# An encoder trunk of two layers: the order of tasks and weight splits chosen by an account of time at build, and a bank of its own for the last 128 columns

## The chip, the cores and the metric

The kernel runs on one core of one Trainium2 chip. The metric is the device time of one execution in microseconds (us); the number given for the kernel before is the median of three runs. TensorE is called PE below, VectorE DVE, ScalarE ACT, GpSimd POOL, and SyncE, which issues the weight loads, SP.

## The reference

```python
D_MODEL = 1024; BATCH = 1; SEQ = 256; DEPTH = 2
HEAD_DIM = 64; D_FF = 2816; GRID_W = 64; WINDOW = 128
...
def swiglu(h, w_gate, w_up, w_down):
    return (jax.nn.silu(h @ w_gate) * (h @ w_up)) @ w_down
...
def even_mixer(h, w_in, q_gain, k_gain, sink, w_out, rope1, rope_axial):
    proj = h @ w_in
    ...
    qa = apply_axial_rope(rms_norm(qa, q_gain), *rope_axial)
    ka = apply_axial_rope(rms_norm(ka, k_gain), *rope_axial)
    oa = global_gqa(qa, ka, va)
    qb = apply_rope(qb, *rope1)
    kb = apply_rope(kb, *rope1)
    ob = windowed_gqa_sink(qb, kb, vb, sink)
    return jnp.concatenate([oa, ob], axis=-1) @ w_out
...
    for layer in range(DEPTH):
        i = layer // 2
        h = rms_norm(x, ffn1_norm[layer])
        x = x + 0.5 * swiglu(h, ffn1_w_gate[layer], ffn1_w_up[layer], ffn1_w_down[layer])
        h = rms_norm(x, mix_norm[layer])
        if layer % 2 == 0:
            x = x + even_mixer(h, even_w_in[i], a_q_norm[i], a_k_norm[i], b_sink[i],
                               even_w_out[i], rope1, rope_axial)
        else:
            x = x + odd_mixer(h, odd_w_qkv[i], c_rel_bias[i], odd_w_out[i], rows)
        h = rms_norm(x, ffn2_norm[layer])
        x = x + 0.5 * swiglu(h, ffn2_w_gate[layer], ffn2_w_up[layer], ffn2_w_down[layer])
    return rms_norm(x, final_norm)
```

The odd mixer is attention within a clamped neighbourhood of a grid of tokens, 16 heads, with a learned bias that is looked up by the relative place. All inputs are float32.

## The kernel before

The 256 tokens are two tiles of 128 rows (`tt` 0 and 1), and `x` stays on chip. There are six stages: feed-forward, even mixer, feed-forward, feed-forward, odd mixer, feed-forward with the final normalisation.

**Products.** Each product of 128 rows of a weight with a tile is done in three matmuls (a triple): each operand is split into a high part and a rest, and high by high, high by rest and rest by high are added (`mm`, L382 to L384). A raw weight block is loaded by SP into one of three buffers (L299). ACT makes its high part `hi` (L390), DVE the rest `lo` (L393). `wp` holds seven such split blocks. The activations are transposed by PE (into banks `tp`) and split in the same way: `th`, `tl` for the normalised `x` (L437, L422), `g_h`, `g_l` for the gated product (L459), `qTb`, `kTaz` and the like for the heads.

**Order.** The engines' lists for PE, ACT, DVE and SP stand as the program is written out. POOL's list is ordered by the framework's own scheduler. Side work (a gated product, a rope, a pair of heads) is a generator, called a task. `tick` runs after each triple; a task says after how many triples it goes on, by numbers written by hand:

```python
GLU_WAIT = 5
KA_WAITS = [2, 5]
EVEN_WAITS = {'a': [[2, 3, 4, 0], [0, 3, 3, 1, 1, 0]], 'b': [[2, 3, 2, 0], [0, 3, 2, 0, 0, 1]]}
```

Weight splits are put in at a fixed number per triple (`RATE` and the like), at most seven blocks ahead; a product whose split isn't made yet makes it on the spot.

**Feed-forward** (`ffn`). Gate and up projections come in chunks of 512 or 384 columns, tile by tile; ACT makes `silu`, DVE the gated product `glu` (L574), and after `GLU_WAIT` triples PE transposes it. The down projection is partly done by Strassen's seven products (`seven`, and `combine`, L671 to L697, whose additions DVE does one by one). The last four blocks of 128 rows of the down projection are held back and done half by half (`use`), so that the additions to `x` (L511) follow each other. In the last stage the second tile's second half is done as 384 and 128 columns, both in one bank `s`.

**Even mixer** (`even`, `attend`). Keys and values of both groups are projected first (bank `s`), then group B's queries (`pj`), then group A's. Keys are rotated by POOL (`kra` for group A, `krb` for B, L869 and L886), then transposed by PE (L933); queries are rotated by DVE (`qr`, L884) and transposed (L459). `pair` then does two heads for each call: scores (L793, L794), maxima by DVE, exponentials by ACT, normalisation by POOL, transposes of `p` (L857) and a copy to `pt` (L753), and the product with the values (L778).

**Odd mixer** (`odd`). The same with `okTz` and `oqT`; POOL builds the bias tables (L1025) from rows that SP loads, DVE adds them to the scores in the pass that takes the maxima (L811), and DVE normalises.

**The end** (`after`). POOL and DVE multiply by the last gain (L1124, L1128), DVE adds up the squares (L1114), POOL raises to the power (L1118), ACT and DVE scale (L1132, L1133), and two queues store.

## Time and profile before

| | us |
|---|---|
| runs | 973.82, 973.82, 975.64 |
| median | 973.82 |
| the profiled execution | 973.97 |
| its span in the trace | 972.2 |
| PE busy | 954.7 |
| DVE busy | 686.2 |
| ACT busy | 554.3 |
| POOL busy | 87.9 |

The profiled execution's own time is 1.77 us longer than its span, which lies outside of what the trace shows. "Busy" is the time in which an engine's records run; PE's matmul records overlap, so PE can be busy all the time and still be fed. A wait is idle time of an engine just before an instruction, with the instruction of another engine that released it. Times within the trace count from the start of the span.

### The profile page before, as it was taken

To read this page: it belongs to the slowest core of one execution; us is meant where nothing else is said; L and a number is where in the kernel's file an instruction comes from. 1 tells how busy PE (TensorE), PEld (TensorE's weight loads), DVE (VectorE), ACT (ScalarE), POOL (GpSimd) and SP (SyncE) were. 2 spreads that over 40 slices of the span, in tenths; PEclk is the share of its full clock that TensorE was granted. 3 is DMA by queue.
4 is the path that set the end of the run, shared out by engine and by line. 5 is a ranking of instruction groups with operands and counts; after the bars stand their busy time and mean duration, and the time that the engine had idled before them with its cause. 6 is when DMAs were issued, how large, how long until landed. Compare 5 with 4: busy or idle time off the path is not lost.

```text
span 972.2 us, 12895 instructions
## 1 busy us (share of the span) xinstructions
PE 954.7 (98%) x4806; PEld 805.7 (83%) x4806; DVE 686.2 (71%) x1095; ACT 554.3 (57%) x960; POOL 87.9 (9%) x152
## 2 busy tenths in 40 slices
PE   9999999998999999999999999999999999999996
PEld 6888998877778888988888899888878888889885
DVE  6665679878857565688866557887869676656796
ACT  7554465576677454555655444648877565445550
POOL 1020000063420000000000000003312000000002
PEclk9999999999999999999999999999999999999998
DMA  8675556563226554646555546465554355545451
GB/s 278 197 254 163 176 191 238 179 174 88 87 87 202 188 171 154 212 160 243 187 174 189 172 158 216 176 257 172 169 158 143 128 176 195 186 158 185 184 195 44
DMA packets 82368, 171.66 MB, mean 177 GB/s; under 512 B 3712, under 2 KB 25216, under 8 KB 82304
## 3 DMA queue, kind: packets, MB, share of 16 engines
q1 hardware_dynamic: 81728, 170.23, 52.9%
q8 instruction: 38, 0.62, 0.3%
q10 hardware_dynamic: 576, 0.59, 0.2%
q14 instruction: 26, 0.21, 0.1%
HBM read 169.76 MB, written 1.05 MB: 176 GB/s over the span
## 4 chain that ended last, share of the span: by engine, by line
PE 93%; ACT 3%; DVE 2%; issue 1%; POOL 1%; DMA 0%; POOLq 0%; ACTq 0%
PE pj L382 14%; PE pj L384 14%; PE pj L383 14%; PE s L382 12%; PE s L384 12%; PE s L383 12%; PE tp L459 3%; PE o L384 2%; PE o L383 2%; PE o L382 2%; PE o L778 1%; PE tp L857 1%; PE tp L437 1%; PE s L793 1%; ACT hi L390 1%
## 5 line engine op out<-in xcount | busy, mean ns | idle before, releaser
L393 DVE TENSOR_TENSOR lo<-raw,hi 128x1024 fp32r<-128x1024 f32 (+2 forms) x388 | 384.1, 1013 | 140.4 <-ACT hi L390 136.6
L390 ACT ACTIVATE hi<-raw 128x1024 fp32r<-128x1024 f32 (+2 forms) x388 | 328.3, 879 | 131.3 <-PE pj L384 106.5
L382 PE MATMUL pj<-hi,th 128*128 128x512 f32 (+1 forms) x512 | 198.4, 388 | 0.0
L384 PE MATMUL pj<-hi,tl 128*128 128x512 f32 (+1 forms) x512 | 193.3, 377 | 0.0
L383 PE MATMUL pj<-lo,th 128*128 128x512 f32 (+1 forms) x512 | 192.9, 377 | 0.1
L382 PE MATMUL s<-hi,th 128*128 128x512 f32 (+1 forms) x400 | 152.5, 381 | 0.0
L384 PE MATMUL s<-hi,tl 128*128 128x512 f32 (+1 forms) x400 | 149.6, 374 | 0.0
L383 PE MATMUL s<-lo,th 128*128 128x512 f32 (+1 forms) x400 | 149.3, 373 | 0.0
L384 PEld LDWEIGHTS pj<-hi,tl 128*128 128x128 f32 x512 | 96.3, 188 | 15.6
L383 PEld LDWEIGHTS pj<-lo,th 128*128 128x128 f32 x512 | 96.7, 189 | 13.4 <-DVE lo L393 0.5
L382 PEld LDWEIGHTS pj<-hi,th 128*128 128x128 f32 x512 | 96.6, 189 | 13.1 <-issue 0.3
L384 PEld LDWEIGHTS s<-hi,tl 128*128 128x128 f32 x400 | 75.4, 188 | 11.1
L383 PEld LDWEIGHTS s<-lo,th 128*128 128x128 f32 x400 | 75.6, 189 | 10.5
L382 PEld LDWEIGHTS s<-hi,th 128*128 128x128 f32 x400 | 75.6, 189 | 10.2
L402 POOL TENSOR_TENSOR rstd<-var,mhalf 128x1 f32<-128x1 f32 (+2 forms) x16 | 15.3, 959 | 586.0 <-ACT th L422 310.2
L574 DVE SCALAR_TENSOR_TENSOR glu<-pj,rstd,silu 128x512 f32<-128x512 f32 (+1 forms) x48 | 33.7, 703 | 41.8 <-PE pj L384 41.8
L382 PE MATMUL s<-hi,g_h 128*128 128x512 f32 (+2 forms) x116 | 45.5, 392 | 2.3 <-DVE x L511 2.3
L384 PE MATMUL s<-hi,g_l 128*128 128x512 f32 (+2 forms) x116 | 44.7, 385 | 0.0
L383 PE MATMUL s<-lo,g_h 128*128 128x512 f32 (+2 forms) x116 | 44.5, 384 | 0.0
L393 DVE TENSOR_TENSOR g_l<-tp,g_h 128x384 fp32r<-128x384 f32 (+1 forms) x48 | 28.8, 599 | 20.8 <-ACT g_h L390 20.8
L390 ACT ACTIVATE shi<-raw 128x1024 fp32r<-128x1024 f32 x16 | 17.0, 1061 | 43.5 <-DVE raw L315 43.5
L422 ACT ACTIVATE th<-tp,mats 128x128 fp32r<-128x128 f32 x88 | 25.2, 371 | 24.7 <-PE tp L437 21.4
(351 smaller groups left out, 1372.2 us busy)
## 6 DMA issues: line engine op xcount, KB each, us to landing
raw<-in_ffn_w_down SPq DMA_DIRECT2D x44, 1024.0 KB, 5.0
raw<-in_ffn_w_up SPq DMA_DIRECT2D x32, 1024.0 KB, 5.1
raw<-in_ffn_w_gate SPq DMA_DIRECT2D x30, 1024.0 KB, 5.1
raw<-in_ffn_w_gate SPq DMA_DIRECT2D x16, 768.0 KB, 4.4
raw<-in_ffn_w_up SPq DMA_DIRECT2D x16, 768.0 KB, 4.5
raw<-in_odd_w_qkv SPq DMA_DIRECT2D x12, 1024.0 KB, 5.1
raw<-in_even_w_in SPq DMA_DIRECT2D x4, 1024.0 KB, 6.3
raw<-in_even_w_out SPq DMA_DIRECT2D x8, 512.0 KB, 5.8
```

The costliest lines, as they stand in the source:

```text
L382: mm(ps, h, wh, start=first, stop=False)
L383: mm(ps, h, wl, start=False, stop=False)
L384: mm(ps, l, wh, start=False, stop=last)
L390: self.nc.scalar.activation(hi, src, AF.Copy)
L393: self.nc.vector.tensor_tensor(lo, src, hi.bitcast(F32), op=ALU.subtract)
L402: nc.gpsimd.tensor_tensor(r[:, :n], v[:, :n], self.mhalf[:, :n], op=ALU.pow)
L422: self.nc.scalar.activation(hi, tb[:, j * P : j * P + P], AF.Copy, scale=gain)
L437: nc.tensor.transpose(tb[:, j * P : (j + 1) * P], self.x[tt][:, b * P : (b + 1) * P], self.ident)
L459: self.nc.tensor.transpose(tb[:, i * P : (i + 1) * P], src[:, i * P : (i + 1) * P], self.ident)
L574: nc.vector.scalar_tensor_tensor(m[:, :w], u[:, :w], self.now.r[tt], s[:, :w], op0=ALU.mult, op1=ALU.mult)
L778: self.nc.tensor.matmul(O[64 * s : 64 * s + 64, i * P : i * P + P], v(b0 + i, s, kc), pT[s][:, i, kc, :], start=(kc == 0), stop=(kc == 1),)
L793: nc.tensor.matmul(S[:, i, :], q, kz[s], start=True, stop=False)
```

## The change

The numbers written by hand go. A class `Clock` reads the instructions as they are written out and adds up rough times for each engine (`cost`, `catch_up`), with the times at which operands are written and buffers come free. A task now yields a `Need`: the engine that goes on with it, the operands it waits for, and a condition. `may` lets it go on when the account has the operands ready: for PE 150 ns ahead of PE's own time, for the others within 400 ns after. `tick` looks at all tasks after each triple; when a triple can't go on, `tick` adds 100 ns of idle PE to the account and tries again. Weight splits are put in whenever there is room and the account has the raw block there (`supply_now`). Banks are counted (`open`, `done`, `has`), and a wait for a bank is one of the conditions.

The second part: where columns 896 to 1024 of the last tile are done apart, their held-back products go to a bank `tp` (`to`), and the addition for 512 to 896 takes in all 512 columns of the bank `s`, with what had been added up before for the last 128; those get a second addition from `tp`. The engines have as many instructions as before, kind by kind.

```diff
 FIT = {"wp": 7, "sum": 3}
-RATE = 0.53
-DOWN_RATE = 0.78
-EVEN_RATE = 0.48
-ODD_RATE = 0.51
+FEW = 4
 
 HELD = 2
 
-X_WAIT = 5
-R_WAIT = 3
-GLU_WAIT = 5
-NAT_WAIT = 2
-ROPE_WAIT = 3
-KB_WAIT = 6
-KA_WAITS = [2, 5]
-QA_WAIT = 9
-EVEN_GAP = {'a': 2, 'b': 2}
-ODD_GAP = [4, 3]
-EVEN_WAITS = {'a': [[2, 3, 4, 0], [0, 3, 3, 1, 1, 0]], 'b': [[2, 3, 2, 0], [0, 3, 2, 0, 0, 1]]}
-ODD_WAITS = [[[2, 4, 5, 4], [2, 4, 5, 3, 1, 2]], [[0, 4, 4, 4], [4, 3, 3, 5, 0, 2]]]
+
+EARLY = 150
+WAIT = 400
+REACH = 1000
...
+class Clock:
...
+        if e == "PE":
+            dt = inst.ins[0].dtype
+            if dt == F32R:
+                t = 9 + 0.426 * n
+            elif dt == F32:
+                t = 109 * n / 128
+            else:
+                t = 0.426 * n
+            return t, t + 165
+        if e == "ACT":
+            t = max(255, 40 + 1.04 * n) + (190 if len(outs) > 1 else 0)
+            return t, t + 70
+        m = n
+        for x in ins:
+            k = 1
+            for _, c in x.ap[1:]:
+                k *= c
+            m = max(m, k)
+        if e == "DVE":
+            return 90 + 1.04 * m, 150 + 1.04 * m
+        t = 650 + 140 * (m - 1) if m <= 8 else 250 + (2.2 if len(ins) > 1 else 1.1) * m
+        return t, t + 20
...
+            begin = max([self.at[e]] + [self.last(self.written, x, e) for x in ins] + [self.last(self.used, x, e) for x in outs])
+            self.at[e] = begin + busy
...
+class Need:
+
+
+    def __init__(self, engine, operands, when=lambda: True, soon=False):
+        self.engine, self.operands, self.when = engine, operands, when
+        self.soon = soon or engine in ("PE", None)
...
+    def has(self, tag):
+
+        if self.open[tag] == BANKS[tag]:
+            return False
+        return self.clock.next_free("acc", tag, BANKS[tag]) + EARLY <= self.clock.at["PE"]
...
+    def may(self, need):
+
+        at = self.clock.at
+        if not need.when():
+            return False
+        if need.engine is None:
+            return True
+        t = self.clock.ready(need.operands)
+        if need.engine == "PE":
+            return t + EARLY <= at["PE"]
+        if at[need.engine] > at["PE"] + REACH:
+            return False
+        return t <= max(at["PE"], at[need.engine]) + WAIT
+
+    def await_parts(self, parts):
+        while self.clock.ready([t for part in parts for t in part]) > self.clock.at["PE"]:
+            self.tick(True)
 
     def finish(self, task):
         while task[1] is not None:
-            self.tick(False)
-
-    def tick(self, supply=True):
-        self.low()
+            self.tick(True)
+
+    def tick(self, idle=False):
+
+        self.clock.catch_up()
+        if idle:
+            self.clock.at["PE"] += 100
+            self.idle += 1
+            assert self.idle < 1000, [task[0] for task in self.tasks]
+        else:
+            self.idle = 0
+        if self.half is not None and self.may(self.need("DVE", self.half[0].parts[0][:, self.half[1]])):
+            self.low()
         for task in list(self.tasks):
-            task[0] -= 1
-            if task[0] <= 0 and task[1] is not None:
-                self.step(task)
-        if supply:
-            self.due += self.rate
-            n = self.whole[0].step() if self.whole else 1
-            if self.due >= n and self.room():
-                self.due = min(self.due - n, n)
-                self.supply()
+            if isinstance(task[0], int) and not idle:
+                task[0] -= 1
+                if task[0] <= 0:
+                    self.step(task)
+            self.go_on(task, True)
+        if sum(self.live.values()) <= FEW:
+            self.supply_now()
+        for task in list(self.tasks):
+            self.go_on(task, False)
+        self.supply_now()
+
+    def go_on(self, task, soon):
+        while task[1] is not None and isinstance(task[0], Need) and (task[0].soon or not soon) and self.may(task[0]):
+            self.step(task)
+
+    def supply_now(self):
+        if self.room() and self.may(self.need("ACT", self.whole[0].raw)) and self.clock.at["DVE"] <= self.clock.at["PE"] + REACH:
+            self.supply()
+            self.clock.catch_up()
...
-            yield GLU_WAIT
+            self.done("pj")
             n = w // P
+            yield self.need("PE", m[:, :w], when=lambda: self.has("tp"))
...
-        def use(f, tt, sl, last=False):
+        def use(f, tt, sl, last=False, to=None):
             while f not in gT[tt]:
-                self.tick(False)
+                self.tick(True)
+            self.await_parts([gT[tt][f]])
             i = sl.start // 512
             at = slice(sl.start % 512, (sl.stop - 1) % 512 + 1)
-            self.mm(Y[tt][i][:, at], gT[tt][f], W[f][i], (tt, i) not in begun, last, at, at.start > 0)
+            ps = Y[tt][i][:, at] if to is None else to[:, : sl.stop - sl.start]
+            self.mm(ps, gT[tt][f], W[f][i], (tt, i) not in begun if to is None else f == held[0], last, at)
...
+                to = self.bank("tp") if sl.start > 512 else None
                 for f in held:
-                    use(f, tt, sl, f == held[-1])
-                at = slice(sl.start % 512, (sl.stop - 1) % 512 + 1)
-                self.start(self.add_to_x(tt, sl, Y[tt][sl.start // 512][:, at], 0.5))
-
-
-    def attend(self, qT, has_q, kT, v, has_v, tag, dest, gap, waits, norm, sink=None, bias=None, scale=None):
+                    use(f, tt, sl, f == held[-1], to)
+                i = sl.start // 512
+                tag = ("o", "pj")[i] if tt == 0 else "s" if to is None else "tp"
+                ps = Y[tt][i] if to is None else to[:, : sl.stop - sl.start]
+                self.start(self.add_to_x(tt, sl, ps, 0.5, tag=tag))
...
-            yield KB_WAIT
+            yield self.need("PE", kr, when=lambda: self.has("tp"))
...
-                    while not has_q(tt):
-                        yield 1
-                    self.start(pair(tt, b0, s))
-                    yield gap
-        while len(dest[NT - 1]) < 4:
-            yield 1
+                    yield self.need(None, when=lambda: qT(tt) is not None and kT(0) is not None)
+                    own = [qT(tt)[b0 + i][s] for i in range(2)] + [kT(b0 + i)[j][s] for i in range(2) for j in range(2)]
+                    yield self.need("PE", *own, when=lambda: self.has("s"))
+                    self.start(pair(n, tt, b0, s))
+                    n += 1
```

How the lists move is shown at three places; line numbers of the changed kernel differ (L565 to L567 are its `mm`, L1154 its transpose of keys).

**Even mixer.** PE's list before, in the first query projection of group B (`pj_2028`), up to the transpose of group A's keys of the first tile (`kra_1969`); this is behind six triples of that projection, of which the last three are shown.

```order
L382 MATMUL pj_2028<-hi_1873,th_1770 128x512
L383 MATMUL pj_2028<-lo_1874,th_1770 128x512
L384 MATMUL pj_2028<-hi_1873,tl_1771 128x512
L382 MATMUL pj_2028<-hi_1926,th_1812 128x512
L383 MATMUL pj_2028<-lo_1927,th_1812 128x512
L384 MATMUL pj_2028<-hi_1926,tl_1813 128x512
L382 MATMUL pj_2028<-hi_1926,th_1815 128x512
L383 MATMUL pj_2028<-lo_1927,th_1815 128x512
L384 MATMUL pj_2028<-hi_1926,tl_1816 128x512
L933 MATMUL tp_2081<-mats,kra_1969 128x128
```

The same place in the changed kernel, from the first product of the projection (there `pj_2032`, and `kra_1967`).

```order
L565 MATMUL pj_2032<-hi_1851,th_1748 128x512
L566 MATMUL pj_2032<-lo_1852,th_1748 128x512
L567 MATMUL pj_2032<-hi_1851,tl_1749 128x512
L565 MATMUL pj_2032<-hi_1851,th_1751 128x512
L566 MATMUL pj_2032<-lo_1852,th_1751 128x512
L567 MATMUL pj_2032<-hi_1851,tl_1752 128x512
L565 MATMUL pj_2032<-hi_1933,th_1754 128x512
L566 MATMUL pj_2032<-lo_1934,th_1754 128x512
L567 MATMUL pj_2032<-hi_1933,tl_1755 128x512
L1154 MATMUL tp_2063<-mats,kra_1967 128x128
```

The transpose stands three triples earlier. POOL's list there before, from the rotation of `ka` of the first tile to its sum `kra`; `kb_2037` is the other group's keys of the second tile, and `kTbx` a copy of transposed keys.

```order
L869 TENSOR_TENSOR t_2_478_2019<-ka_1968,gtab 128x128
L869 TENSOR_TENSOR t_2_479_2020<-ka_1968,gtab 128x2x16 x4
L489 CAST kTbx_425_1851<-kTbz_423_1849 64x128
L489 CAST kTbx_426_1852<-kTbz_424_1850 64x128
L869 TENSOR_TENSOR t_2_483_2041<-kb_2037,tab 128x128
L869 TENSOR_TENSOR t_2_484_2042<-kb_2037,tab 128x2x32 x2
L886 TENSOR_TENSOR kra_1969<-t_2_478_2019,t_2_479_2020 128x128
```

And POOL's list in the changed kernel, from the two copies on:

```order
L682 CAST kTbx_434_1866<-kTbz_432_1864 64x128
L682 CAST kTbx_435_1867<-kTbz_433_1865 64x128
L1150 TENSOR_TENSOR ka_1966<-ka_1966,rstd_1984 128x128
L1089 TENSOR_TENSOR t_2_472_1987<-ka_1966,gtab 128x128
L1089 TENSOR_TENSOR t_2_473_1988<-ka_1966,gtab 128x2x16 x4
L1089 TENSOR_TENSOR t_2_483_2041<-kb_2037,tab 128x128
L1089 TENSOR_TENSOR t_2_484_2042<-kb_2037,tab 128x2x32 x2
L1106 TENSOR_TENSOR kra_1967<-t_2_472_1987,t_2_473_1988 128x128
```

The copies of `kTbx` moved up by three places; the two products from `kb_2037` stand ahead of `kra` in both.

**Odd mixer.** DVE's list before, from the first group's first pair of scores on: `s_6547` is the first pair's scores, `bias_6264` and `bias_6270` the first two tables, `oqT_1556` the split of the second tile's queries.

```order
L811 ISA p_6568,m_6567<-s_6547,bias_6264 128x256
L811 ISA m_6567 128x1
L811 ISA p_6568,m_6567<-s_6547,bias_6270 128x256
L811 ISA m_6567 128x1
L816 TENSOR_SCALAR m_1554_6571<-m_6567 128x2
L393 TENSOR_TENSOR lo_6561<-raw_6115,hi_6560 128x512
L393 TENSOR_TENSOR oqT_1556_6586<-tp_6576,oqT_1556_6586 64x512
L393 TENSOR_TENSOR oqT_1557_6587<-tp_6576,oqT_1557_6587 64x512
```

In the changed kernel, from the second pair of scores on (the first stands just ahead), with the second and third pair's scores (`s_6564`, `s_6570`) and the third and fourth table (`bias_6291`, `bias_6297`):

```order
L1031 ISA p_6584,m_6583<-s_6564,bias_6279 128x256
L1031 ISA m_6583 128x1
L1031 ISA p_6584,m_6583<-s_6564,bias_6285 128x256
L1031 ISA m_6583 128x1
L1036 TENSOR_SCALAR m_1560_6587<-m_6583 128x2
L1031 ISA p_6590,m_6589<-s_6570,bias_6291 128x256
L1031 ISA m_6589 128x1
L1031 ISA p_6590,m_6589<-s_6570,bias_6297 128x256
L1031 ISA m_6589 128x1
L1036 TENSOR_SCALAR m_1563_6593<-m_6589 128x2
L576 TENSOR_TENSOR oqT_1566_6608<-tp_6598,oqT_1566_6608 64x512
```

The pass with the third and fourth table now stands ahead of the split of `oqT`; it came later before.

**The end.** DVE's last additions to `x` before, from the second tile's first half on:

```order
L511 SCALAR_TENSOR_TENSOR x_86<-s_8766,x_86 128x512
L1114 ISA sq_9168,v_9169<-x_86 128x512
L1114 ISA v_9169 128x1
L511 SCALAR_TENSOR_TENSOR x_86<-s_8767,x_86 128x384
L1114 ISA sq_9185,v_9186<-x_86,v_9169 128x384
L1114 ISA v_9186 128x1
L511 SCALAR_TENSOR_TENSOR x_86<-s_8767,x_86 128x128
L1114 ISA sq_9201,v_9202<-x_86,v_9186 128x128
L1114 ISA v_9202 128x1
```

and in the changed kernel:

```order
L706 SCALAR_TENSOR_TENSOR x_86<-s_8761,x_86 128x512
L1333 ISA sq_9168,v_9169<-x_86 128x512
L1333 ISA v_9169 128x1
L706 SCALAR_TENSOR_TENSOR x_86<-s_8762,x_86 128x512
L1333 ISA sq_9185,v_9186<-x_86,v_9169 128x384
L1333 ISA v_9186 128x1
L706 SCALAR_TENSOR_TENSOR x_86<-tp_9188,x_86 128x128
L1333 ISA sq_9202,v_9203<-x_86,v_9186 128x128
L1333 ISA v_9203 128x1
```

The last 128 columns' products now stand in `tp_9188`, and the addition ahead of them is 512 columns wide.

304 lines of the change are left out of this document (212 added, 92 removed).

## The prediction

> **What bounds the kernel now.** I read the page's first lines, then the busy time by stage, then the waits of the tensor engine, and last the timelines at the places where it waits.
>
> ```profile
> span 972.2 us, 12895 instructions
> PE 954.7 (98%) x4806; PEld 805.7 (83%) x4806; DVE 686.2 (71%) x1095; ACT 554.3 (57%) x960; POOL 87.9 (9%) x152
> PE 93%; ACT 3%; DVE 2%; issue 1%; POOL 1%; DMA 0%; POOLq 0%; ACTq 0%
> 0.00:25.00 25.00, 22.73 (x88) 16.19 (x89) 15.53 (x33) 18.89 (x41) 2.76 (x8) 1.00 0.85 281
> 25.00:181.00 156.00, 156.00 (x756) 134.88 (x755) 106.74 (x125) 81.02 (x108) 7.08 (x22) 1.00 0.61 203
> 181.00:290.00 109.00, 102.51 (x605) 80.60 (x604) 83.33 (x198) 73.38 (x198) 40.07 (x82) 0.98 0.40 116
> 660.00:775.00 115.00, 114.40 (x670) 93.85 (x669) 91.51 (x238) 83.94 (x193) 28.56 (x30) 1.00 0.52 163
> 956.00:973.00 17.00, 8.03 (x43) 6.78 (x42) 11.08 (x23) 1.12 (x2) 4.90 (x4) 0.80 0.17 63
> ```
>
> The reader is to see that PE carries 93% of the chain and is busy 954.7 of 972.2 us. The first number behind a window's length is PE's busy time. The first feed-forward stage (25 to 181) has no idle PE at all. The even mixer (181 to 290) has 109.00 - 102.51 = 6.5 us idle, the odd mixer (660 to 775) 0.6, the end 9.0, the start 2.3. Since the change leaves every matmul in place, it can win only from these 17.5 us and from stretches at half clock, and most of the 9.0 at the end is the last tile's normalisation and the store, which stay.
>
> ```profile
> PE s L382 <- DVE x L511: 2.3, 1, 2.3
> PE s L793 <- DVE qTb L393: 2.0, 1, 2.0
> PE tp L857 <- ACT pt L753: 1.4, 2, 0.8
> PE pj L382 <- DVE t L869: 1.2, 1, 1.2
> PE tp L459 <- DVE qr L884: 1.2, 1, 1.2
> ```
>
> These single waits are what the new order can move: the first is at the end, one of the two for `pt` is in the odd mixer, the rest are in the even mixer.
>
> **Even mixer, up to the first scores.** Before, PE reaches the transpose of `kra` after six triples of products of the first query projection.
>
> ```profile
> 207.71 0.39 PE L384 MATMUL pj<-hi,tl 128*128 128x512 f32 x1
> 210.43 0.33 PE L933 MATMUL tp<-mats,kra 128*128 128x128 f32 x1 [0.29 <-POOL kra L886]
> 211.53 0.33 PE L933 MATMUL tp<-mats,krb 128*128 128x128 f32 x1
> 214.90 0.39 PE L384 MATMUL pj<-hi,tl 128*128 128x512 f32 x1
> 216.45 0.63 PE L459 MATMUL tp<-mats,qr 128*128 128x128 f32 x4 [1.16 <-DVE qr L884]
> 218.30 0.27 PE L933 MATMUL tp<-mats,kra 128*128 128x128 f32 x1
> 220.56 0.36 PE L793 MATMUL s<-kTbz,qTb 128*128 128x256 f32 x1 [1.99 <-DVE qTb L393]
> ```
> ```profile
> 207.98 1.54 POOL L869 TENSOR_TENSOR t<-kb,tab 128x128 f32<-128x128 f32 x3
> 209.48 0.90 POOL L886 TENSOR_TENSOR kra<-t,t 128x128 f32<-128x128 f32 x1
> ```
>
> Start to start, 512-column products are 0.227 us apart, a triple 0.68. In the new order `kra` is transposed after three triples, so PE is there at 207.71 + 0.23 = 207.94 on this clock. But POOL's list still has the rotation of the second tile's `kb` ahead of it, and POOL delivers `kra` at 209.48 + 0.90 = 210.38 as now. The wait there **grows** from 0.45 (210.43 less 209.98, three triples after 207.94) to about 2.4. Behind it the next transposes are farther off: `krb` five triples on (211.53 comes 1.10 after 210.43, where a triple and two switches between kinds of 0.09 take 0.86: its 0.24 go), `qr` five more. DVE needs the whole projection before `qr`; that ends about 214.2, `qr` is there about 216.6, PE comes at about 217.5, so the 1.32 at 216.45 (216.45 less 215.13) goes. Between these transposes and the scores now stand four triples, 2.72 us; ACT's and DVE's splits of `qTb`, behind two small `kTa` splits, need about 2.3. So the 2.15 before 220.56 (less 218.41) goes too. Sum: 2.4 - 0.45 - 0.24 - 1.32 - 2.15 = **-1.8**. The ends are -4.2, were POOL to deliver `kra` when PE comes, and 0, were `qTb` late by the 1.8 again.
>
> **The clock.**
>
> ```profile
> 215.12:218.54 3.42, 2.26 (x12) 1.58 (x11) 2.35 (x5) 1.38 (x3) 0.40 (x1) 1.00 0.32 65
> 218.54:221.95 3.41, 1.42 (x10) 1.25 (x10) 2.84 (x5) 2.13 (x5) 0.73 (x2) 1.00 0.17 36
> 221.95:225.36 3.41, 3.41 (x13) 2.74 (x12) 1.83 (x5) 1.89 (x4) 0.20 (x1) 0.50 1.07 242
> ```
>
> In stretches of 3.41 us, one with 1.99 us idle was followed by one at clock 0.50, and one with 1.16 idle was not. Half a clock over 3.41 us costs 1.7. The new wait of 2.4 for `kra`, and the one of 2.3 in the odd mixer (below), lie between a whole stretch and its halves, by where the grid falls: each about one in two. I take **one** of them to be followed by half clock, as one is now: 0 in the sum, with -1.7 for none and +1.7 for both.
>
> [...]
>
> **Rest of the even mixer.**
>
> ```profile
> 230.00:290.00 60.00, 57.02 (x391) 44.00 (x390) 43.90 (x109) 43.46 (x118) 21.72 (x41) 1.00 0.29 88
> 715.07 0.69 DVE L393 TENSOR_TENSOR lo<-raw,hi 128x512 fp32r<-128x512 f32 x1
> ```
>
> Here 60.00 - 57.02 = 3.0 us are idle. Walked through by hand with the durations of the trace, the new order loses the waits for `pt` and for a bank read by DVE, and gets others: two waits for a bank near the second and third pair of scores, and four splits of the output projection's weights that now stand directly ahead of their product, where before other work lay between. Each such split costs up to the 0.69 of its DVE half: 4 x 0.69 = 2.8. The ends are -3.0 and +2.8; I take **-0.6**, near the middle, on the side of the walk.
>
> **Odd mixer.**
>
> ```profile
> 682.73 9.11 POOL L1025 TENSOR_TENSOR bias<-rows,mats 128x384 f32<-128x384 f32 x8 [5.12 <-DMA rows<-in_c_rel_bias]
> 684.84 0.28 PE L793 MATMUL s<-okTz,oqT 128*128 128x256 f32 x1
> 688.74 0.42 DVE L811 CUSTOM_DVE_ANT_1 p<-s,bias 128x256 f32<-128x256 f32 x1
> 691.07 1.39 DVE L393 TENSOR_TENSOR oqT<-tp,oqT 64x512 fp32r<-64x512 f32 x2
> 724.21 0.66 PE L857 MATMUL tp<-mats,p 128*128 128x128 f32 x4 [0.60 <-ACT pt L753]
> ```
>
> POOL builds the first group's eight bias tables until 682.73 + 9.11 = 691.84; the first scores need only the first ones. In the new order DVE's list has three pairs of scores in a row and the third takes the last tables; behind it stands the split of the second tile's queries (`oqT`), which the fifth pair of scores needs. PE is there after four triples, sixteen score matmuls (0.12 apart) and four transposes, 684.84 + 2.72 + 1.9 + 0.5 = 690.0. DVE is ready at 691.84 + 0.42 + 0.2 + 0.7 = 693.2. The wait is 3.2, or less if the tables start earlier: their rows are fetched behind a weight load that waits for its buffer, and that buffer is freed a little sooner in the new order. I take 0.9 for it (worked out from the new place of the split that frees it; ends 0 and 2.6): wait 2.3. In exchange the 0.76 us before 724.21 (less 723.45) go. Sum **+1.5**, ends -0.2 and +2.4.
>
> **The end.**
>
> ```profile
> 958.54 1.28 DVE L675 TENSOR_TENSOR x<-x,glu 128x512 f32<-128x512 f32 x2
> 962.26 0.58 DVE L1133 TENSOR_SCALAR shi<-shi,r 128x704 f32<-128x704 f32 x1 [0.44 <-POOL r L1118]
> 964.70 0.33 PE L382 MATMUL s<-hi,g_h 128*128 128x128 f32 x1 [2.29 <-DVE x L511]
> 966.35 0.29 DVE L511 SCALAR_TENSOR_TENSOR x<-s,x 128x128 f32<-128x128 f32 x1 [0.63 <-PE s L384]
> ```
>
> PE's last twelve products wait for DVE to read the bank that they share. In a bank of their own they run at once, and PE's 2.29 us go. But what ends last is DVE's list, and DVE idles only 0.63 for these products. That 0.63 goes. The list is also one of the two `x` additions at 958.54 shorter ahead of the first tile's last add, 0.6, and the 384-column add becomes 512 wide, about 0.13 longer. Sum 0.63 + 0.6 - 0.13 = **-1.1**. Ends: -2.3, if all of PE's wait counted, and -0.1, if the wait for POOL's `r` (0.44 at 962.26) takes the 0.6 and half of the rest.
>
> **The start.**
>
> ```profile
> 23.39 0.39 PE L382 MATMUL pj<-hi,th 128*128 128x512 f32 x1
> 23.87 0.50 PE L383 MATMUL pj<-lo,th 128*128 128x512 f32 x1
> ```
>
> 0.48 where 0.227 is the step: a split that came directly ahead of its product. The new order makes it earlier: **-0.3**, ends -0.4 and 0.
>
> **Feed-forward stages: nothing.** Their weights are split at least eighteen products, 4 us, ahead of their use in both orders. What moves is the transposes of the gated product.
>
> ```profile
> 49.04 0.39 PE L384 MATMUL pj<-hi,tl 128*128 128x512 f32 x1
> 49.47 0.75 DVE L574 SCALAR_TENSOR_TENSOR glu<-pj,rstd,silu 128x512 f32<-128x512 f32 x1 [0.93 <-PE pj L384]
> ```
>
> Now they come eighteen products after the projection's last one (first tile); then six, that is 49.27 + 1.36 = 50.63. DVE's product ends at 49.47 + 0.75 = 50.22, and if PE follows it by 0.05, as it followed POOL at 210.43, or a little more, the cover is about 0.3 us at each of 24 places. DVE idled 0.93 ahead of this one. I cost it at 0.
>
> **The sum.** -1.8 + 0 - 0.6 + 1.5 - 1.1 - 0.3 = -2.3 us, against the profiled execution's 973.97: **971.7**. That execution stands 0.15 above the median of 973.82, which needs no correction.
>
> **The rivals.**
>
> *The clock stays full*: neither new wait fills one stretch. The two waits are hardly longer than the 1.99 that was enough, and a grid line inside either one splits it. -2.3 - 1.7: 970.0. [...]
>
> *The account does all that it says*: the odd wait is hidden since the tables come 2.6 earlier, the rest of the even mixer halves its idle time, the clock stays full. -1.8 - 1.7 - 1.5 - 0.8 - 1.1 - 0.3 = -7.2: 966.8. Against it speaks POOL, whose order the account does not set.
>
> *The new waits give it back*: the tables come no earlier (+0.9) and both waits are followed by half clock (+1.7). -2.3 + 2.6 = +0.3: 974.3.
>
> *The change does not do what it says*: the rough account puts tasks so that the old waits return one place on, and only the end and the start win: -1.4, or 972.6.
>
> *Slower, by the gated product's transposes*: the cover of 0.3 us is eaten where DVE is still in a weight split (1024 columns, about 1.2) when the projection ends. From a lateness of 0.3 on, PE stands still at each of the 24 places. Half a split late, PE stands 0.6 - 0.3 = 0.3 at a place; with a full split, 0.9. At all 24 places that is between 7.2 and 21.6; I take the lower. -2.3 + 7.2 = +4.9: 978.9. For it: DVE has 71% of the span. Against: it idles ahead of 24 of its 48 gated products.
>
> **How the numbers follow.** Forecast 0.35; full clock 0.20; all that it says 0.13; given back 0.14; not what it says 0.06; slower 0.12. What a measurement can tell from no change is about 0.2%, 1.95 us, so faster means below 971.87. The forecast's own spread (970 to 973.5) gives 0.19 faster and 0.16 same; with the others, faster 0.19 + 0.20 + 0.13 = 0.52, same 0.16 + 0.11 + 0.06 = 0.33, slower 0.12 + 0.03 = 0.15. The range reaches from the full effect, 966.8, to a little over the case that gives it back, 975.5; what is left out is the slower case and a little below.
>
> **What would show it.** In the changed kernel's waits the rows for `qTb` and `qr` are gone, the one for `kra` has 2 us or more, a row of the odd mixer for `oqT` (or `p`) has 1 to 3, and none for L511 stands at the end. The feed-forward stages stay without idle PE. The prediction is wrong if the wait for `kra` is short, if gated-product transposes show waits, or if the end moves by the full 2.3.

## The result and the profile after

| | before | after |
|---|---|---|
| median, us | 973.82 (973.82 to 975.64) | 987.3 (986.3 to 990.18) |
| profiled execution and its span, us | 973.97, 972.2 | 986.57, 984.8 |
| granted clock, mean | 0.995 | 0.997 |
| ratio after / before | | 1.0138 [1.0113, 1.0164] |

The change made the kernel 1.4% slower; forecast were 971.7 and a range up to 975.5. The page of the changed kernel, first lines and chain:

```profile
span 984.8 us, 12886 instructions
PE 956.9 (97%) x4806; PEld 804.9 (82%) x4806; DVE 694.6 (71%) x1095; ACT 556.3 (56%) x960; POOL 88.9 (9%) x152
PE 75%; DVE 13%; ACT 6%; issue 3%; DMA 2%; POOL 1%; SPq 0%; POOLq 0%; ACTq 0%; DVEq 0%
```

PE does the same 4806 matmuls in about the same busy time, but its share of the chain falls from 93% to 75%, and DVE's rises from 2% to 13%: PE now stands behind DVE. Busy time by stage, in the form of the rows of before (length, then PE's busy time), for the even mixer, a feed-forward stage with the changes of stage on both sides of it, and the odd mixer:

```profile
181.00:290.00 109.00, 100.39 (x601) 78.81 (x600) 86.59 (x202) 75.39 (x204) 42.39 (x83) 1.00 0.40 116
470.00:660.00 190.00, 188.49 (x903) 160.70 (x903) 131.60 (x173) 100.56 (x148) 1.10 (x2) 1.00 0.52 183
660.00:775.00 115.00, 108.64 (x633) 87.48 (x631) 88.71 (x232) 81.84 (x192) 27.79 (x30) 0.99 0.43 138
```

PE's idle time in the odd mixer is 115.00 - 108.64 = 6.4 us, 0.6 before; in the even mixer 8.6, 6.5 before; and 1.5 from 470 to 660, where before PE was busy all the time (190.00 of 190.00 us). PE's longest waits:

```profile
PE tp L647 <- ACT nat L1263: 3.0, 1, 3.0
PE tp L623 <- DVE x L706: 2.9, 11, 0.6
PE s L1013 <- ACT p L1055: 2.4, 3, 0.9
PE tp L1154 <- POOL kra L1106: 2.2, 1, 2.2
PE pj L566 <- DVE lo L576: 2.0, 3, 1.0
PE s L1013 <- DVE m L1031: 1.8, 1, 1.8
PE pj L565 <- DVE x L706: 1.7, 1, 1.7
```

Gone are the waits for `qTb`, `qr`, `t` and the last `x`. New are the odd mixer's `nat` (the scaled queries that PE transposes) and `m` (the pass that adds the bias and takes the maximum), eleven at the changes of stage (`x` at L623), one in the odd output projection (L565), and in the even mixer three for a bank of scores that ACT still reads (`p`) and, in its output projection, two for a late `lo`.

Where the 12.6 us of span went: at each place the start of the matmul that has the same amount of matmul work behind it in both traces, after less before. This counts a wait whole, where a row of waits leaves out the 0.16 us by which a matmul's drawn 0.39 exceeds its step of 0.227.

| stretch | us | forecast |
|---|---|---|
| start | -0.5 | -0.3 |
| within the feed-forward stages | 0 | 0 |
| changes of stage: to even, between two feed-forwards, to odd | +1.5, +2.15, +1.75 | not in it |
| even mixer | -0.6 | -2.4 |
| odd mixer: first group, second group, output projection | +5.1, +2.8, +1.8 | +1.5 |
| end | -1.4 | -1.1 |

**First group of the odd mixer.** From the timelines of POOL, DVE, ACT and PE of the changed kernel, then of DVE in the kernel before:

```profile
686.41 9.47 POOL L1247 TENSOR_TENSOR bias<-rows,mats 128x384 f32<-128x384 f32 x8 [5.12 <-DMA rows<-in_c_rel_bias]
686.49 1.41 DVE L576 TENSOR_TENSOR oqT<-tp,oqT 64x512 fp32r<-64x512 f32 x2 [3.11 <-ACT oqT L573]
687.92 6.27 DVE L576 TENSOR_TENSOR lo<-raw,hi 128x512 fp32r<-128x512 f32 x5
694.12 0.14 DVE L1261 TENSOR_SCALAR rs<-rstd 128x1 f32<-128x1 f32 x1
694.38 0.69 ACT L1263 ACTIVATE nat<-pj,rs 128x512 f32<-128x512 f32 x1 [5.18 <-DVE rs L1261]
695.12 1.11 PE L647 MATMUL tp<-mats,nat 128*128 128x128 f32 x4 [2.95 <-ACT nat L1263]
...
698.59 1.41 DVE L576 TENSOR_TENSOR oqT<-tp,oqT 64x512 fp32r<-64x512 f32 x2 [0.88 <-ACT oqT L573]
```
```profile
684.28 2.19 DVE L393 TENSOR_TENSOR lo<-raw,hi 128x512 fp32r<-128x512 f32 x2
686.38 0.14 DVE L1040 TENSOR_SCALAR rs<-rstd 128x1 f32<-128x1 f32 x1
```

Read the middle: `rs`, one number per row and 0.14 us of work, stands on DVE's list behind five weight splits that nothing needs yet. ACT has idled 5.18 us for it and PE 2.95. Before, two splits stood there. And a split takes 6.27 / 5 = 1.25 us here, and 2.19 / 2 = 1.10 before, against the 0.69 of other rows: both stretches lie under POOL's bias tables. The account prices a split of 512 columns at 90 + 1.04 x 512 ns, 0.62 us. Behind the wait PE's clock is halved for a stretch of 3.41 us (windows of the changed kernel; the first number behind the length is PE's busy time, the last but two the clock):

```profile
691.33:694.74 3.41, 0.83 (x5) 0.36 (x3) 3.38 (x7) 0.36 (x1) 3.41 (x3) 1.00 0.90 298
694.74:698.15 3.41, 3.03 (x11) 2.76 (x12) 2.87 (x13) 3.37 (x8) 1.14 (x2) 0.50 0.02 6
```

The eleven matmuls from 695.12 on take 3.04 us, up to 698.16. At full clock the same ones come to 1.58: four transposes 0.42 (before, 687.38 to 687.80), four scores 0.12 apart, three products 0.227 apart. So the group's 5.1 are, from start to start, the wait for `nat` (3.1), half clock (1.5) and a wait for `oqT` (0.5; its row has 0.3).

**Second group and output projection**, changed kernel:

```profile
735.78 8.60 POOL L1247 TENSOR_TENSOR bias<-rows,mats 128x384 f32<-128x384 f32 x8 [2.38 <-DMA rows<-in_c_rel_bias]
740.06 5.46 DVE L576 TENSOR_TENSOR lo<-raw,hi 128x512 fp32r<-128x512 f32 x5
746.48 0.36 PE L1013 MATMUL s<-okTz,oqT 128*128 128x256 f32 x1 [1.76 <-DVE m L1031]
...
777.99 2.59 DVE L576 TENSOR_TENSOR lo<-raw,hi 128x1024 fp32r<-128x1024 f32 x2 [0.83 <-ACT hi L573]
780.49 1.28 DVE L706 SCALAR_TENSOR_TENSOR x<-pj,x 128x512 f32<-128x512 f32 x2
781.23 0.50 PE L565 MATMUL pj<-hi,ot_00h 128*128 128x512 f32 x1 [1.65 <-DVE x L706]
```

The same shape twice more: five splits ahead of the pass that frees the scores' bank, and two wide ones ahead of the addition that frees `pj`.

**A change of stage**, PE of the changed kernel, then of the kernel before:

```profile
470.75 0.66 PE L623 MATMUL tp<-mats,x 128*128 128x128 f32 x4 [0.59 <-DVE x L706]
474.40 0.66 PE L623 MATMUL tp<-mats,x 128*128 128x128 f32 x4 [0.23 <-DVE x L706]
```
```profile
470.95 0.60 PE L437 MATMUL tp<-mats,x 128*128 128x128 f32 x4
474.14 0.60 PE L437 MATMUL tp<-mats,x 128*128 128x128 f32 x4
```

Before, two more triples stood between the products that end a part of `x` and its transposes. Now PE comes 0.2 to 0.6 us before DVE's addition has ended, four times at each of the changes between two feed-forwards and to the odd mixer, three times at the change to the even mixer. DVE's list of the changed kernel shows what the addition stands behind:

```profile
472.62 1.13 DVE L612 SCALAR_TENSOR_TENSOR tl<-tp,mats,th 128x128 fp32r<-128x128 f32 x4 [0.73 <-ACT th L607]
473.66 0.68 DVE L706 SCALAR_TENSOR_TENSOR x<-pj,x 128x512 f32<-128x512 f32 x1
```

The splits `tl` need the transposes that PE has just made, and the addition that the next transposes need stands behind them. So one transpose follows another by 3.65 us (470.75, 474.40), where before they are 3.19 apart (470.95, 474.14).

**The end**, changed kernel: PE's last product, and DVE behind it without an idle stretch.

```profile
977.42 0.28 PE L567 MATMUL tp<-hi,g_l 128*128 128x128 f32 x1
978.14 0.89 DVE L1333 CUSTOM_DVE_ANT_0 sq<-x,v 128x384 f32<-128x384 f32 x1
978.97 0.28 DVE L706 SCALAR_TENSOR_TENSOR x<-tp,x 128x128 f32<-128x128 f32 x1
```

### The profile page after: what moved, and what is told of

Same layout as the page of the kernel before. It is cut to its first block, busy times and chain, and to the rows that moved or that the text cites. A ratio compares the mean times of both kernels' runs of the same rounds, so it can differ in the third digit from the quotient of the medians.

```text
span 984.8 us, 12886 instructions
## 1 busy us (share of the span) xinstructions
PE 956.9 (97%) x4806; PEld 804.9 (82%) x4806; DVE 694.6 (71%) x1095; ACT 556.3 (56%) x960; POOL 88.9 (9%) x152
## 4 chain that ended last, share of the span: by engine, by line
PE 75%; DVE 13%; ACT 6%; issue 3%; DMA 2%; POOL 1%; SPq 0%; POOLq 0%; ACTq 0%; DVEq 0%
PE pj L565 13%; PE pj L566 12%; PE pj L567 12%; PE s L567 9%; PE s L565 9%; PE s L566 9%; DVE lo L576 5%; PE tp L647 2%; PE o L998 2%; PE tp L1077 1%; DMA raw<-in_ffn_w_gate 1%; ACT th L607 1%; ACT shi L573 1%; DVE tl L612 1%; DVE x L706 1%
## 5 line engine op out<-in xcount | busy, mean ns | idle before, releaser
L565 PE MATMUL pj<-hi,th 128*128 128x512 f32 (+1 forms) x512 | 198.2, 387 | 0.0
L567 PE MATMUL pj<-hi,tl 128*128 128x512 f32 (+1 forms) x512 | 193.2, 377 | 0.0
L565 PE MATMUL s<-hi,th 128*128 128x512 f32 (+1 forms) x400 | 151.8, 380 | 0.0
L567 PE MATMUL s<-hi,tl 128*128 128x512 f32 (+1 forms) x400 | 149.2, 373 | 0.0
L567 PEld LDWEIGHTS pj<-hi,tl 128*128 128x128 f32 x512 | 96.2, 188 | 15.8
L565 PEld LDWEIGHTS pj<-hi,th 128*128 128x128 f32 x512 | 96.6, 189 | 13.7 <-issue 0.5
L567 PEld LDWEIGHTS s<-hi,tl 128*128 128x128 f32 x400 | 75.2, 188 | 10.8
L565 PEld LDWEIGHTS s<-hi,th 128*128 128x128 f32 x400 | 75.5, 189 | 10.1
L585 POOL TENSOR_TENSOR rstd<-var,mhalf 128x1 f32<-128x1 f32 (+2 forms) x16 | 12.6, 790 | 587.6 <-DVE var L583 394.1
L573 ACT ACTIVATE g_h<-tp 128x384 fp32r<-128x384 f32 (+1 forms) x48 | 25.2, 526 | 59.1 <-PE tp L647 51.1
L789 ACT ACTIVATE quarters<-tp 128x256 f32<-128x256 f32 x16 | 6.1, 384 | 86.3 <-PE tp L647 86.3
L565 PE MATMUL s<-hi,g_h 128*128 128x512 f32 (+1 forms) x112 | 44.0, 393 | 0.0
L567 PE MATMUL s<-hi,g_l 128*128 128x512 f32 (+1 forms) x112 | 43.5, 388 | 0.0
L566 PE MATMUL s<-lo,g_h 128*128 128x512 f32 (+1 forms) x112 | 43.4, 387 | 0.0
```

The costliest lines, as they stand in the source:

```text
L565: mm(ps, h, wh, start=first, stop=False)
L566: mm(ps, h, wl, start=False, stop=False)
L567: mm(ps, l, wh, start=False, stop=last)
L573: self.nc.scalar.activation(hi, src, AF.Copy)
L585: nc.gpsimd.tensor_tensor(r[:, :n], v[:, :n], self.mhalf[:, :n], op=ALU.pow)
```

## The experiments

Times of before on the chips of the three batches: 974.69 (e1 to e4), 974.16 (e5 to e8), 974.3 (e9, e10). Ratios are to these. Added lines move the line numbers by two or three (L647 becomes L650).

**e1: five triples ahead of the transposes of `x` again.**

```diff
+X_WAIT = 5
...
-        yield self.need("PE", self.x[tt][:, half * 512 : half * 512 + 512], when=lambda: self.has("tp"))
+        due = self.ticks + X_WAIT
+        yield self.need("PE", self.x[tt][:, half * 512 : half * 512 + 512], when=lambda: self.ticks >= due and self.has("tp"))
```

> The changed kernel, but the transposes of x for the next stage may come only five triples after they could (as the kernel before had it). Theory T (each transpose, its split on ACT and DVE, and the next addition to x form a chain of 3.65 us per half, against 3.2 us of PE's products): the eleven waits of PE for x at L706, 2.9 us in all, and the issue gaps around them go, and three changes of stage get 1.5, 2.2 and 1.8 us back: about 5 us less than the changed kernel, near 982. Rival (the additions are late because of the combination's additions ahead of them, whatever comes after): the waits stay and the time is the changed kernel's, 987.

990.29 us, ratio 1.0164 [1.0149, 1.0179]. The stalls it aims at go or shrink: by the measure of the table above the three changes of stage lose 0, 0.4 and 1.1 us (1.5, 2.15 and 1.75 in the changed kernel). But the account starts from other times after that and orders the even mixer anew, which now loses 5.4 us, where the changed kernel won 0.6. Waits of PE there:

```profile
PE tp L1157 <- POOL kra L1109: 2.7, 1, 2.7
PE pj L569 <- DVE oTa12l L578: 1.8, 1, 1.8
```

The place of the transposes is a cause of those stalls; mending it alone doesn't bring the time back, and the 982 expected were missed.

**e2: `rs` of each tile at its first use, whichever part comes first.**

```diff
-            if i == 0 and rs[tt] is None:
+            if rs[tt] is None:
```

> The changed kernel, but the 128x1 product rs (the query's scale) is made when the keys are copied, so that it no longer stands behind five weight splits on DVE. Theory A (that place is what the first group of the odd mixer waits for): the 3.0 us wait of PE for nat goes, with the stretch at half clock behind it, and DVE's third pass with bias, which needs the last tables, becomes the next wait, so that PE waits about 2 us for oqT or a bank: 2 to 4 us less than the changed kernel, 983 to 985. Theory B (the prediction's: only the last bias tables hold the group): nothing changes, since PE would wait for the tables all the same, 987.

990.39 us, 1.0154 [1.013, 1.0177]. The wait for `nat` is gone, and the first group gains only 0.6: the five splits are still there, and the next small operation behind them is the pass of the scores.

```profile
691.27 6.25 DVE L576 TENSOR_TENSOR lo<-raw,hi 128x512 fp32r<-128x512 f32 x5
...
698.47 0.36 PE L1013 MATMUL s<-okTz,oqT 128*128 128x256 f32 x1 [2.52 <-DVE m L1031]
```

So the wait isn't `rs`'s own; it is 6.3 us of splits, and whatever comes behind them is late. The total is no lower than the changed kernel's, against the 983 to 985 expected: in this execution PE fell to half clock behind the wait for `kra` too, in an even mixer that the edit doesn't touch (last section).

**e3: splits only while the account has DVE at least 1 us behind PE.**

```diff
-        ... self.clock.at["DVE"] <= self.clock.at["PE"] + REACH:
+        ... self.clock.at["DVE"] <= self.clock.at["PE"] + -1000:
```

> The changed kernel, but a weight split is put in ahead of need only while the account has DVE 1 us behind PE, where the changed kernel allows it 1 us ahead: two splits stand ahead of rs instead of five, and fewer ahead of the scores of the second group. Theory A (splits put in too early hold DVE's small urgent work): the waits for nat (3.0) and for m and oqT (1.8 and 0.9) shrink to under 1 us each and the odd mixer gets 4 to 7 us back; waits for lo or hi may come up elsewhere, 0 to 3 us: 981 to 985. Theory B (bias tables): the first group's wait stays at about 3, and the whole at 986 to 988.

1083.18 us, 1.1118 [1.1101, 1.1134], 100 us above what was expected: the splits are now late everywhere.

```profile
PE pj L566 <- DVE lo L576: 23.8, 26, 2.8
```

The `nat` wait did fall to 0.6, but what the splits cost by being early can't be had back by making all of them late. Nothing more is taken from it.

**e4: POOL's additions of the odd bias replaced by fills, priced alike in the account**, so that the lists of PE, ACT and DVE stay as they are. The bias is left out of the computation. The fills wait for no rows, and none runs beside the five splits.

```diff
-        t = 650 + 140 * (m - 1) if m <= 8 else 250 + (2.2 if len(ins) > 1 else 1.1) * m
+        t = 650 + 140 * (m - 1) if m <= 8 else 250 + (2.2 if len(ins) > 1 or m == 384 else 1.1) * m
...
-            nc.gpsimd.tensor_tensor(bias[:, i], runs, near, op=ALU.add)
+            nc.gpsimd.memset(bias[:, i], 0.0)
```

> The changed kernel with the same lists on PE and DVE, but POOL fills the bias tables with zeros instead of adding rows and masks: the odd mixer's bias is left out. Theory A with contention (DVE's splits run at 1.25 us instead of 0.69 while POOL adds): the five splits ahead of rs take about 3.5 instead of 6.3 us, the wait for nat falls from 3.0 to about 0.4, no half clock follows, the second group's wait for m falls from 1.8 to under 0.5: 5 to 7 us less than the changed kernel, 980 to 982. Rival (the splits are slow for another reason, such as the late arrival of hi): their durations stay at 1.25 and the time is 986 to 988. Theory B (tables late) would give the same total as contention, but leave the splits at 1.25 each.

984.31 us, 1.010 [1.0076, 1.0124].

```profile
689.46 3.10 DVE L576 TENSOR_TENSOR lo<-raw,hi 128x512 fp32r<-128x512 f32 x5
```

The same five splits take 3.10 instead of 6.27 us. The first group loses 3.2 less than in the changed kernel (a wait of 1.7 for `oqT` is then the next), the second 2.35 less: so 5.5 of the odd mixer's 9.7 go with POOL's additions, the stretch at half clock behind the first wait among them. The kernel before wasn't run without them; PE idled 0.6 us in its odd mixer, so it had little to win there. This execution's span is 3.9 below that of the changed kernel, since the stretches ahead of the odd mixer came out 1.5 to 1.9 longer.

**e7: the real tables, but the first four built in the feed-forward stage ahead**, where DVE's list has room; DVE's list is the same, operation for operation.

```diff
+            self.start(self.early_tables(a["c_rel_bias"][0]))
             self.phase(self.ffn)
...
-            bias = [self.bias_table(rel, g * 8 + 2 * b) for b in range(4)]
+            bias = self.early[4 * g : 4 * g + 4]
+            bias += [self.bias_table(rel, g * 8 + 2 * b) for b in range(len(bias), 4)]
```

> The changed kernel with DVE's list the same, operation for operation, but the odd mixer's first four bias tables are built one stage earlier, during the feed-forward stage; the second group's are built where they were. Theory A with contention: the five splits ahead of rs take 3.1 to 3.5 us instead of 6.3, as with the tables left out, and the first group gets back about 3 us, plus 1.7 where half clock followed; the second group's waits (1.8 and 0.6) stay, since its tables are built beside its splits as before: 982 to 984. In the feed-forward stage the splits beside the adds take twice as long and PE waits for nothing there. Theory B (tables arrive late) says the same of the first group's total, but not of the splits' durations.

984.66 us, 1.0105 [1.0091, 1.0119]. POOL first, in the feed-forward stage; then DVE and PE in the odd mixer:

```profile
532.54 1.84 POOL L1255 TENSOR_TENSOR bias<-rows,mats 128x384 f32<-128x384 f32 x2 [8.59 <-DMA rows<-in_c_rel_bias]
...
688.41 3.10 DVE L576 TENSOR_TENSOR lo<-raw,hi 128x512 fp32r<-128x512 f32 x5
...
696.65 0.39 PE L1013 MATMUL s<-okTz,oqT 128*128 128x256 f32 x1 [1.68 <-DVE oqT L576]
```

No wait of PE appears where POOL now builds the tables. Splits at 0.62 each, `nat` in time, the first group 3.2 better than in the changed kernel; the second group, whose tables are built where they were, keeps its wait for `m` (2.1), and in this execution half clock follows it. That is e4's reading with nothing left out of the computation.

**e6: the additions to `x` written out right behind their products.**

```diff
-        if nxt.n < 6:
-            yield self.soon("DVE", ps)
+        if tag is None:
+            yield
```

> The changed kernel, but the additions to x are written out right after their products instead of as a task that waits for its turn, so that on DVE an addition stands ahead of the splits tl of the transposes before it where it stood behind. Theory T (each half of a stage's end is a chain of transpose, th, tl, addition, transpose of 3.65 us against PE's 3.2): the waits of PE for x at L706 before the transposes shrink from 2.9 us in eleven to under 1, and the changes of stage cost about 2 us instead of 5.4: 983 to 985. Rival (PE's order is to blame, the transposes stand too close behind the additions in any case): the waits stay at 2 to 4 us and the time at 986 to 988.

987.82 us, 1.0141 [1.0116, 1.0165].

```profile
474.70 0.66 PE L623 MATMUL tp<-mats,x 128*128 128x128 f32 x4 [1.37 <-DVE x L706]
...
786.18 0.50 PE L565 MATMUL pj<-hi,ot_00h 128*128 128x512 f32 x1 [0.28 <-DVE x L706]
```

Two answers. In the output projection the wait falls from 1.65 to 0.28: there the splits ahead of the addition were the cause. At the change between two feed-forwards the loss stays at 2.1, but in other parts, and this doesn't show that DVE's list is without blame. The first addition isn't moved: it stands behind the combination's passes, with no idle time of DVE between, and PE's wait for it is 1.37, 0.59 in the changed kernel (1.12 in e2, which has the changed kernel's order there: it differs by execution). The second stays behind the splits `tl`. The third now stands ahead of them, PE's list moves with it, and the third and fourth transposes wait no more. The profiled execution is the slowest of the four (985.07 to 991.56); it has two stretches in a row at half clock behind the wait for `nat`.

**e5: the kernel before, with only the second part of the change**, the bank `tp` for the last 128 columns and the addition 512 wide.

> The kernel before with the second part of the change alone: the last 128 columns' held-back products go to a bank of their own, and the addition ahead of them is 512 columns wide. By the prediction's term for the end (only DVE's 0.63 us of idle time counts, less 0.13 for the wider addition; the 0.6 of the combination's shorter list belongs to the order): 0.5 us less than before. Rival (PE's whole wait of 2.3 counts): 2.3 us less. Second rival (the wait for POOL's power takes its place): no change. In the trace PE's wait for x at L511 is gone in every case.

972.69 us (11 runs, 972.08 to 973.14), 0.9983 [0.9974, 0.9992]: the fastest version of the study, ahead of both kernels.

```profile
964.65 0.89 DVE L1115 CUSTOM_DVE_ANT_0 sq<-x,v 128x384 f32<-128x384 f32 x1
965.47 0.28 DVE L512 SCALAR_TENSOR_TENSOR x<-tp,x 128x128 f32<-128x128 f32 x1
```

PE's 2.3 us go whole, and the span loses 0.9, of which 0.7 lie at the end: DVE's list was what ended last, and it idled 0.63 there.

**e8: e5, and by hand the one thing that the account gets right in the even mixer**, the transposes of the rotated `qr` three triples later (`ROPE_WAIT` 3 to 6).

> The kernel before with the bank of its own, and ROPE_WAIT 6 in place of 3: in the even mixer the transposes of the rotated queries of group B come three triples later, and with them the first scores. By the prediction's even mixer term (waits of 1.32 for qr and 2.15 for qTb that go when more triples stand ahead of them, with no wait for kra growing): 1.5 to 2.7 us less in the even mixer, 1.7 more where half clock followed the wait for qTb, and 0.5 at the end: 970 to 972 against 973.8. Rival (the waits come back one place on, as scores that wait for a bank or as the last heads' results): 973 to 975.

973.36 us, 0.9991 [0.9982, 1.0]. The wait for `qr` goes and that for `qTb` falls to 0.9, and others come:

```profile
PE pj L382 <- DVE t L870: 1.8, 1, 1.8
PE s L794 <- ACT p L836: 1.0, 3, 0.4
```

Slower than e5 by 0.7 us, against the 970 to 972 expected, and although no stretch of this execution is at half clock in the even mixer: a wait that is taken away comes back one place on.

**e9: e1's five triples only in the stages on either side of the change between two feed-forwards; e10: e9 with e7's tables and e2's `rs`.**

Against e1:

```diff
-        due = self.ticks + X_WAIT
+        due = self.ticks + (X_WAIT if i in (3, 4) else 0)
```

> The changed kernel, with the five triples ahead of the transposes of x only where a feed-forward stage follows a feed-forward stage and where the odd mixer follows (two of five changes of stage), so that nothing moves in the even mixer. Theory T (the transposes stand two triples closer behind the additions than in the kernel before, and PE waits out DVE's list there): the seven waits of 0.4 to 0.8 us at 470 to 481 and 657 to 668 go; those two changes of stage cost 2.2 + 1.8 us in the changed kernel and about 0.5 + 0.7 then: 2 to 3 us less, 984 to 985. Rival (the time comes back in the odd mixer or elsewhere, as it came back in the even mixer when all changes of stage were moved): 986 to 988.

> The same, and the odd mixer's first four bias tables a stage earlier, and rs made with the keys. If the causes found add up (change of stage 2 to 3, the first group's contention 2.7 to 3.2): 981 to 983. What is left over the kernel before would then be the first change of stage (1.5), the first group's and the second group's waits for DVE (about 1.9 and 2.9), and the odd mixer's output projection (1.8). Rival (the first group's other waits take the place of the one removed, as with rs alone): 984 to 985.

e9: 988.17 us, 1.014 [1.0124, 1.0156]. Against before, the change between the two feed-forwards now costs nothing, and that to the odd mixer 1.15, all of it at a transpose of `nat`. Yet the total doesn't fall: up to 40 us this execution lost 1.5 to before, 1.1 of it waiting for one gated product, and half clock cost 1.9 in the even mixer. e10: 983.06 us, 1.009 [1.0073, 1.0107]: the first group's loss falls from 5.1 to 0.75. It is the best of the repaired orders, and its span is still 10.6 above that of before: about 4.1 up to the end of the even mixer (0.7 waiting for the same gated product, the first change of stage, half clock), 1.15 at the change to the odd mixer, 0.75 in its first group, 4.2 in the second (a wait for `m` of 2.4 with half clock behind it) and 1.8 in the output projection, with 1.4 won at the end.

## Why the prediction was wrong, point by point

**Odd mixer: forecast +1.5, measured +9.7.** This is the step that failed most. It asked when POOL would deliver the last tables ("DVE is ready at 691.84 + 0.42 + 0.2 + 0.7") and took DVE to be free but for that; it didn't walk DVE's own list up to that place. POOL was done with the last tables at 695.88, ahead of the third pair's pass at 696.73; what was late was the head of that list: five splits, at 1.25 us each, ahead of `rs` and the passes. e2 shows that the block of splits, not the one operation behind it, is the cause; e4 and e7 show that half of the block's length is POOL's. Both facts could have been read before: the order gives the five splits, and the row at 684.28 gives 1.10 us a split beside POOL's tables. The second group (e4: 2.35 of 2.8) and the output projection (e6: 1.4 of 1.8) are the same mechanism, and the prediction had no term for waits there.

The traces narrow this down: a split `lo`, made from `raw` and `hi`, goes from 0.62 us (e7, 3.10 / 5) to 1.25 beside POOL's additions, while `oqT`, 64x512, which is made from the bank `tp` that PE wrote, takes 1.41 / 2 = 0.70 beside them (686.49) and the same without them (698.59). Why one is slowed and the other is not was not shown.

**Changes of stage: not in the sum, measured +5.4.** The prediction put the feed-forward stages at nothing: weights are split early enough, and the gated product has 0.3 us of cover. That held in the profiled execution of after, which has no wait for a gated product and only one of 0.33 us for a split (at 24.75), so its slower rival fell. The cover is thin, though: e2, e9 and e10, whose order is the same there, each wait once for one gated product, at about 36 us, for 0.6, 1.1 and 0.7 us. What the prediction did not ask is the same question of the transposes of `x`, which the new order moves two triples, six matmuls or 1.4 us, nearer to DVE's additions. e1 takes most of the stall away by moving them back. e6 takes it away for the one addition that it moves ahead of the splits `tl`, though PE's list moved with it there; how much DVE's passes ahead of the first addition cost was not tried.

**Even mixer: forecast -2.4, measured -0.6.** Up to the first scores the mechanism was right: the wait for `kra` grew as POOL's list said (2.4 forecast; its row has 2.23, which is 2.4 from start to start), and those for the second `krb`, for `qr` and for `qTb` went. New is a wait for the first tile's `krb` (0.32, or 0.5 from start to start), so it came to about -1.3 against -1.8. The half clock that before had here is absent from the profiled execution of after (1.00 in the window 181 to 290, 0.98 before), which is worth -1.7; it came in the odd mixer instead. So the rest, forecast at -0.6, cost about -0.6 + 1.3 + 1.7 = +2.4, within its ends of -3.0 and +2.8, at the far one. This term was mis-sized, not its mechanism. The rows of waits behind the first scores add up to 2.8 in before and to 5.3 in after, and the new ones are those that the prediction's walk named: 2.4 for the scores' bank, at three pairs, and 2.1 for late splits in the output projection. The walk gave a price only to the second kind. e1 and e8 show that such waits move with any edit.

**End: forecast -1.1, measured -1.4**, and by e5 -0.7 for the bank alone, from the 0.63 of DVE's idle time less 0.13 for the wider addition and 0.14 gained on the sum of squares. Right, with the reason given: PE's 2.3 us did not count. **Start: -0.3 and -0.5**; in the other executions with the same order there, the first 40 us came out between 0.3 less and 1.5 more than in before, so this settles nothing.

**The rivals.** The dearest one put its loss at 24 small places of the feed-forward stages; the loss came in three large ones of the odd mixer and in eleven at changes of stage. The one in which new waits give the gain back, 974.3, had the right sign, and half clock did follow the odd mixer's wait; but it let the tables be late, and they were not what PE waited for. That the clock term came out at about nothing, half clock once before and once after, is luck of where the two waits fell.

## What to carry to other kernels

An order chosen by an account is as good as its prices where one engine slows another: here a split was priced at 0.62 us, took 1.25 beside POOL, and made late every small operation queued behind it. To judge such a change, walk the list of each engine that PE waits for at the start of a stage, and ask what bulk work stands ahead of the smallest operation that others need; and check every producer whose consumer moves nearer, not only the ones that waited before. Take the local parts of a change alone: here the bank by itself was the gain, and the new order hid it.

## What the runs showed of the hardware

**DVE and POOL.** The 1.25 us are a mean; single records say more. A split and an addition of POOL that run beside each other in the odd mixer of after:

```profile
688.73 1.43 DVE L576 TENSOR_TENSOR lo<-raw,hi 128x512 fp32r<-128x512 f32 x1
689.58 1.39 POOL L1247 TENSOR_TENSOR bias<-rows,mats 128x384 f32<-128x384 f32 x1
```

Alone, such a split takes 0.69 us (before, at 694.83) and such an addition 0.94 (after, at 735.78). Beside each other, one split and one addition are done in each 1.35 us: splits begin at 688.73, 690.09, 691.44 and 692.78, additions at 688.22, 689.58, 690.93 and 692.27. Alone, splits follow each other by 0.60 us (before, three in 1.89 from 697.70 on) and additions by 0.90 (after, two in 1.84 from 735.78 on), together 1.50: little is won by running them at the same time.

**The clock.** A wait of a given length is not followed by half clock each time. The wait for `kra` (2.2 us in each row, with the same order up to there) was followed by it in e2, e9 and e10 (mean granted clock of these executions 0.993, 0.993 and 0.995), and not in after, e4 and e7 (0.997, 0.998 and 0.998). The stretches of 3.41 us stand on a grid (in before, half clock begins at 221.95 and again at 966.06, which is 218 x 3.413 us later), and what differs is how the grid cuts the wait. In e2 (first two rows) one stretch holds 3.41 - 1.17 = 2.24 us without PE work, and the next is at half clock; in after (last two) it holds 1.83, and the next is at full clock:

```profile
210.61:214.02 3.41, 1.17 (x7) 0.67 (x6) 1.38 (x2) 1.05 (x4) 3.41 (x10) 1.00 0.87 198
214.02:217.43 3.41, 3.41 (x10) 2.64 (x10) 2.51 (x7) 2.21 (x5) 1.99 (x5) 0.50 0.57 117
```
```profile
210.05:213.46 3.41, 1.58 (x8) 1.32 (x9) 1.08 (x4) 1.17 (x4) 2.60 (x7) 1.00 1.08 229
213.46:216.88 3.42, 3.42 (x17) 2.78 (x16) 3.27 (x8) 1.60 (x5) 2.72 (x6) 1.00 0.26 81
```

That is how the prediction read it. With the grid laid through a trace's first stretch at half clock, and away from the start and the end, stretches at full clock with 2.58 us (after, from 691.33), 1.99 (before, from 218.54) and 1.97 (e6, from 697.41) without PE work were followed by half clock, and those with 1.92 (e1, from 695.39) and 1.83 (after, from 210.05) by full clock. One with 1.78 was followed by half clock nevertheless (e9, the wait for `m` before 747.65), so the idle time alone doesn't settle it there.
